# Attention's value products as plain float32 on halves of the array, row sums by ones on its quarters

## The chip, the cores and the metric

The kernel runs on one core of one Trainium2 chip. TensorE (PE, with its weight loader PEld) multiplies into PSUM, eight banks of 128 x 512 float32; VectorE (DVE) and ScalarE (ACT) read and write PSUM and SBUF; GpSimd (POOL) works on SBUF alone. Transfers (DMA) are issued from SyncE's queue (SP) or from GpSimd's. The metric is the device time of one execution in microseconds (us), the median of several runs.

## The reference: one layer for a prompt and eight short streams

One encoder layer is applied to a prompt of 2048 frames and to 8 streams of 16 new frames with 1024 cached ones. A modulated norm and one input projection give two groups of channels. Group A is a gated convolution of width 31 with a layer norm and a swish. Group B is attention with 8 heads of 64 channels and a forget gate: queries and keys are normed, and the logit of query t and key s has the sum of the log forget values between them added. The two are joined, projected and added to the input, and a gated feed-forward part follows. In the prompt's attention, cut to what matters:

```python
s = einsum('bqhd,bkhd->bhqk', q, k) * HEAD_DIM ** -0.5
s = s + (cum_q[..., :, None] - cum_k[..., None, :])
s = where(k_pos <= q_pos, s, -1e30)
p = softmax(s)
out = einsum('bhqk,bkhd->bqhd', p, v)
```

Everything is float32, and the results must have nearly float32's precision.

## The kernel before

**Two kinds of product.** A float32 operand can be given to TensorE as plain float32, or as fp32r, a reduced form that streams faster. Where the kernel wants speed and precision it splits an operand x into two fp32r halves, hi (ACT's copy of x) and lo = x - hi (DVE or GpSimd), and adds three products, hi*hi, hi*lo, lo*hi. The helper `parts_of` (lines 1158 to 1162) does the split, so the split of every operand appears in the profile under lines 1160 and 1161 and must be told apart by its tile name.

**Stages.** `project_u_v`, then `project_q_k` (norms, queries and keys, already split, go to the DRAM tensors `q_d` and `k_d`), `attention` (lines 778 to 827), `project_out`, and the feed-forward part `ffn_up` and `ffn_down`.

**Attention.** `STEPS` are 16 steps: 4 pairs of heads p, times 4 blocks qb of 512 queries. In a step, scores lie with the keys on the 128 partitions and the 512 queries along the row. A step has 4 * qb + 4 key tiles (kt) of 128 keys, for each of two heads h; the last four cross the diagonal, and only 512, 384, 256 and 128 of their query columns are computed. One score (a unit of the step's loop) is two fp32r products into a bank of the tag "u" (three banks), the first with the hi parts K1 and Q1, the second with K2 and Q2, which hold the rest and, in rows from `AUX` = 96, the maxima to be subtracted; a third product adds the mask on the diagonal.

`attend` (lines 954 to 1006) turns a score into weights: ACT's exp into `ef` (line 981), the split of `ef` into the two halves of `e` (line 986: ACT's copy, then DVE or, for every third, GpSimd), and later the products of `value` (lines 962 to 965): three fp32r products of 128 stationary columns for each head. The stationary operand is V's 64 channels beside 64 columns of ones, so each head has a bank of its own (tag "tr"), in which 64 rows are the result and 64 the row sums. V is split in `load` (lines 896 to 911). At the end of a step (lines 995 to 1006) ACT copies the four half banks out, computes 1 / sum as exp(-ln), DVE refines that in three operations, multiplies, and SP's queue stores into `cat_d`.

`score_maxima` (lines 913 to 943) runs ahead of the scores: for each 128 queries and 512 keys one product (line 934) into a bank of the tag "cv" (two banks) and one DVE maximum (line 937). `spread_maxima` (lines 945 to 952) transposes a step's maxima and multiplies them with a constant `bm` into Q2's aux rows (line 950). A score is pinned behind a maximum (lines 974 and 975): at least `AHEAD` = 32 and up to 40 ahead of its own number. `attention` emits 48 ahead (`LEAD`).

**Order of the work.** `weave` mixes the generators of a step: its scores, the loads for the next, the maxima, and from the third step on a slice of `background`: layer norms of the convolution (`conv_norm`) and then the streams' attention (`sample_setup`, `sample_batch`), all in one PSUM bank, "lane". They use plain float32 products, many of them on quarters of the array's columns with `tile_position` (lines 716, 1073, 1107). A scheduler with a timeline of its own puts each engine's instructions in order by priority; `later` shifts the priority (`MAXIMA_BY`, `BACK_BY`), and `after` pins one instruction behind another on one engine. Keys, queries (lines 889, 891, 903, 927) are loaded through GpSimd's queue; V and nearly all else through SP's. Both queues work in order: an issue that waits holds those behind it.

## Time and profile before

| | us |
|---|---|
| median of 3 runs | 2819.75 (2818.45 to 2822.88) |
| the profiled execution's own time | 2814.3 |
| its span, first to last instruction | 2812.5 |
| attention, first exp to last value product | 625.9 to 1197.6 |
| first product of the output projection | 1200.5 |

A row of a group reads: line, engine, operation, out <- in, shapes, count | busy us, mean ns of one | idle time of its engine ahead of it and what ended most of that. A plain float32 product is recorded as two MATMULs; "128*32" is the part of the array in rows and columns. A row of a timeline is the start, the time from there to the end of the merged instructions, and what they are. A row of waits is the waiting engine and line <- what released it: us in total, times, the longest. PE's busy time includes each product's way through the array after its last column has entered, so two products that follow each other overlap in it; the distance between starts tells what one costs.

### The profile page before, as it was taken

What the parts mean: (1) busy time and instruction counts of PE and PEld (TensorE: products, weight loads), DVE (VectorE), ACT (ScalarE), POOL (GpSimd) and SP (SyncE); (2) the same over time, 40 slices, a digit from 0 to 9 for tenths busy, and PEclk for the clock granted to TensorE, in tenths of its full rate; (3) what the DMA queues carried; (4) which work ended last, traced back from release to release, by engine and by line L of the source; (5) the groups of instructions that cost most, each with busy time, mean ns of one, the idle gap of its engine ahead of it and who ended that gap; (6) DMA issues with size and microseconds to landing.
All of it is one profiled execution on the core that took longest, in us unless ns stands there. A gap on an engine that the chain in (4) does not pass through costs nothing. (4 is left out here: it accounts for less than half of the span.)

```text
span 2812.5 us, 48566 instructions
## 1 busy us (share of the span) xinstructions
PE 2718.6 (97%) x16536; PEld 2515.7 (89%) x16536; DVE 2161.9 (77%) x4235; ACT 1428.7 (51%) x2812; POOL 503.9 (18%) x685
## 2 busy tenths in 40 slices
PE   7999999999989999999999999999999999999999
PEld 6999988866667777698999989999999999999999
DVE  2798898989888787546397989877887778666765
ACT  4443323357776777744354446444554446555552
POOL 3454411243333222214201110000000000000000
PEclk9999999979999999999999999999999999999999
DMA  8753657673334766365576869866786769788883
GB/s 325 249 192 107 191 209 267 182 204 109 101 95 128 203 179 189 130 215 179 181 259 209 294 215 308 268 221 218 233 287 214 226 190 319 244 284 257 271 255 116
DMA packets 389960, 599.24 MB, mean 213 GB/s; under 512 B 47136, under 2 KB 250048, under 8 KB 387664
## 3 DMA queue, kind: packets, MB, share of 16 engines
q1 hardware_dynamic: 375248, 570.73, 62.8%
q0 software_dynamic: 14464, 25.42, 3.9%
q8 instruction: 130, 2.13, 0.3%
q14 instruction: 118, 0.97, 0.1%
HBM read 421.97 MB, written 174.08 MB: 212 GB/s over the span
## 5 line engine op out<-in xcount | busy, mean ns | idle before, releaser
L1456 PE MATMUL z<-rT,rW 128*128 128x360 f32 (+1 forms) x8316 | 1383.3, 328 | 5.5 <-ACT rW L1160 1.4
L1456 PEld LDWEIGHTS z<-rT,rW 128*128 128x128 f32 x8316 | 1378.7, 188 | 8.1 <-ACT rW L1160 2.4
L1160 ACT ACTIVATE rW<-rR 128x512 fp32r<-128x512 f32 x714 | 434.4, 617 | 386.8 <-PE z L1456 272.1
L1161 DVE TENSOR_TENSOR rW<-rR,rW 128x512 fp32r<-128x512 f32 x714 | 479.5, 676 | 154.5 <-ACT rW L1160 151.3
L700 DVE SCALAR_TENSOR_TENSOR cv<-cu,cpar,cv 128x384 f32<-128x384 f32 x580 | 311.6, 614 | 2.8 <-ACT cv L698 2.8
L964 PE MATMUL pv<-e,V 128*128 128x512 f32 (+3 forms) x960 | 268.9, 388 | 14.1 <-DVE e L1161 6.3
L964 PEld LDWEIGHTS pv<-e,V 128*128 128x128 f32 x960 | 167.9, 194 | 71.7 <-DVE e L1161 14.6
L937 DVE TENSOR_REDUCE M<-mx 128x1 f32<-128x512 f32 (+2 forms) x320 | 188.7, 603 | 50.2 <-PE mx L934 31.7
L981 ACT ACTIVATE ef<-s 128x512 f32<-128x512 f32 (+3 forms) x320 | 167.1, 532 | 116.7 <-PE s L979 47.1
L512 PE MATMUL z<-hqx,wqh 128*128 128x384 f32 (+1 forms) x768 | 196.6, 333 | 1.0 <-DVE logf L347 1.0
L1160 ACT ACTIVATE rT<-traw 128x360 fp32r<-128x360 f32 (+1 forms) x315 | 149.1, 501 | 91.7 <-DMA traw<-gt_d 62.9
L1161 DVE TENSOR_TENSOR rT<-traw,rT 128x360 fp32r<-128x360 f32 (+1 forms) x315 | 157.6, 531 | 45.0 <-ACT rT L1160 44.7
L1161 POOL TENSOR_TENSOR e<-ef,e 128x512 fp32r<-128x512 f32 (+3 forms) x106 | 127.2, 1200 | 347.4 <-ACT e L1160 180.7
L1160 ACT ACTIVATE e<-ef 128x512 fp32r<-128x512 f32 (+3 forms) x320 | 175.5, 567 | 4.0
L1161 DVE TENSOR_TENSOR e<-ef,e 128x512 fp32r<-128x512 f32 (+3 forms) x214 | 149.1, 704 | 35.4 <-ACT e L1160 34.4
L512 PEld LDWEIGHTS z<-hqx,wqh 128*128 128x128 f32 x768 | 135.7, 188 | 18.9 <-issue 15.3
L934 PE MATMUL mx<-K,Q 96*128 96x512 f32 (+2 forms) x320 | 134.3, 427 | 17.5 <-DVE M L937 11.3
L1144 PE MATMUL acc<-ch,woh 128*128 128x360 f32 (+1 forms) x384 | 127.4, 333 | 10.0 <-ACT ch L1160 4.6
L1384 DVE TENSOR_TENSOR rR<-rR 128x512 f32<-128x512 f32 (+1 forms) x136 | 93.4, 707 | 50.9 <-DMA rR<-w_down 44.1
L973 PE MATMUL s<-Q,K 128*128 128x512 f32 (+3 forms) x320 | 125.8, 393 | 3.4 <-ACT ef L981 3.4
L1144 PE MATMUL acc<-ch,wol 128*128 128x360 f32 (+1 forms) x384 | 126.9, 331 | 0.0
L512 PE MATMUL z<-hqx,wql 128*128 128x384 f32 (+1 forms) x384 | 126.4, 329 | 0.0
(306 smaller groups left out, 3935.4 us busy)
## 6 DMA issues: line engine op xcount, KB each, us to landing
rR<-sup_d SPq DMA_DIRECT2D x176, 256.0 KB
rR<-w_gate SPq DMA_DIRECT2D x132, 256.0 KB
traw<-gt_d SPq DMA_DIRECT2D x154, 180.0 KB
rR<-w_down SPq DMA_DIRECT2D x104, 256.0 KB
rR<-sdn_d SPq DMA_DIRECT2D x96, 256.0 KB
rR<-w_up SPq DMA_DIRECT2D x88, 256.0 KB
sup_d<-rR SPq DMA_DIRECT2D x88, 256.0 KB
wa<-w_ada SPq DMA_DIRECT2D x16, 1024.0 KB
```

What stands on the lines that cost most here:

```text
L512: nc.tensor.matmul(z[:, :n], w[:, m], x[:, :n], start=(c == 0 and k == 0), stop=(c == CB - 1 and k == 2))
L700: self.pin(nc.vector.scalar_tensor_tensor(dst, src, w, acc[i], ALU.mult, ALU.add))
L934: self.mx.append(nc.tensor.matmul(mx[:, :w], Q2[0:AUX, h, j * P:(j + 1) * P], K2[kb][0:AUX, h, :w], start=True, stop=not diag))
L937: nc.vector.tensor_reduce(M[:, i, kb:kb + 1], mx[:, :w], AX.X, ALU.max)
L964: nc.tensor.matmul(z[h][:, off:], V[kt // 4][:, v, kt % 4, h:h + 2, :].rearrange("p b c -> p (b c)"), e[:, x, off:], start=(kt == 0 and i ...
L973: first = nc.tensor.matmul(s[:, off:], K1[kb][:, h, sl], Q1[:, h, off:], start=True, stop=False)
L981: self.last_piece = nc.scalar.activation(ef[:, off:], s[:, off:], AF.Exp)
L1144: self.nc.tensor.matmul(z[:, :n], w[:, m], y, start=(first and i == 0 and k == 0), stop=(last and i == len(terms) - 1 and k == 2))
L1160: copy = self.nc.scalar.activation(hi, raw, AF.Copy)
L1161: engine.tensor_tensor(lo, raw, f32(hi), ALU.subtract)
L1384: nc.vector.tensor_tensor(t, x, y, op)
L1456: nc.tensor.matmul(z, W[:, x, m], t[:, y, :w], start=(k == 0 and i == 0), stop=(k == n - 1 and i == 2))
```

## The change

- Value products: `e` is ACT's exp in float32, not split; V is loaded in float32 straight into its tile, not split. Per key tile one plain float32 product for each head, with 64 stationary columns, head 0 on the array's columns 0 to 63, head 1 on 64 to 127, into one bank.
- Row sums: after every second key tile, for the two tiles and the two heads, a plain float32 product with 32 columns of ones on one quarter of the array each (in steps with qb = 0 both tiles use the same two quarters), into a second bank.
- Order: the products of a key tile are pinned behind the scores of the key tile two later, sums behind products, the next scores and maxima behind those. The last products of a step run in the next step's first key tiles.
- End of a step: ACT copies the product bank (`zc`) and the sums (`sm`). Through GpSimd's queue the sums go to DRAM and come back with the 512 queries spread over the partitions, DVE adds and takes the reciprocal (in the next step, 8 scores later), they go to DRAM again and come back broadcast to 64 rows for each head; GpSimd multiplies, and its queue stores. The very last step instead spreads the sums by a product, and DVE takes the reciprocal of 128 x 512.
- Maxima: `spread_maxima` copies the transposed rows and sends 8 rows by SP's queue to row 96 of Q2, one aux row instead of 8; `bm` goes. `MAXIMA_BY` goes from -300 to 30, the lead from up to 40 to up to 42.
- Keys and queries are loaded through SP's queue instead of GpSimd's.
- Newton steps after exp(-ln/2): one instead of two, in `project_q_k` and `conv_norm`.
- Background: loads of cached keys and of the streams' bias are issued one piece earlier, more yields, and its first products are pinned behind a score's last product (`behind`).

```diff
-MAXIMA_BY, BACK_BY = -300, 1000
+MAXIMA_BY, BACK_BY = 30, 1000
...
-            newton_rsqrt(nc, y, zp.tile([P, NB], F32, tag="t", name="rt", bufs=1)[:, :n], v, 2, self.pin)
+            newton_rsqrt(nc, y, zp.tile([P, NB], F32, tag="t", name="rt", bufs=1)[:, :n], v, 1, self.pin)
...
-            nc.gpsimd.dma_start(K2[0:HD + 2], rows[HD:])
+            nc.sync.dma_start(f32(K2[0:HD + 2]), rows[HD:])
...
-            nc.gpsimd.dma_start(k1, rows[0:P])
+            nc.sync.dma_start(f32(k1), rows[0:P])
...
-        nc.gpsimd.dma_start(Q1, self.q_d[2 * p:2 * p + 2, :, t].rearrange("h r t -> r h t"))
+        nc.sync.dma_start(f32(Q1), self.q_d[2 * p:2 * p + 2, :, t].rearrange("h r t -> r h t"))
...
-        hi, lo = (v[:, i, :, 0:3:2, :] for i in range(2))
-        self.after(self.parts_of(hi, lo, raw.rearrange("p t (h e) -> p t h e", h=2), nc.vector), self.last_piece)
...
                     self.mx.append(nc.tensor.matmul(mx[:, :w], Q2[0:AUX, h, j * P:(j + 1) * P], K2[kb][0:AUX, h, :w], start=True, stop=not diag))
+                    if self.last_product:
+                        self.after(self.mx[-1], self.last_product)
...
-        for h in range(2):
-            nc.vector.tensor_tensor(Q2[r, h, :].rearrange("r (j q) -> r j q", j=4),
-                                    pz[r, :].unsqueeze(1).broadcast_to([8, 4, P]),
-                                    self.bm[r, h, :].unsqueeze(2).broadcast_to([8, 4, P]), ALU.mult)
+        m = self.lp.tile([P, P], F32R, tag="mrow", name="mrow", bufs=1)
+        nc.vector.tensor_copy(m[r], pz[r])
+        for i in range(8):
+            nc.sync.dma_start(f32(Q2[AUX:AUX + 1, i // 4, i % 4 * P:(i % 4 + 1) * P]), f32(m[AUX + i:AUX + i + 1]))
...
+        def values(kt, off, es):
+            if kt == 0:
+                z.append(self.bank("tr", "pv"))
+            for h in range(2):
+                product = nc.tensor.matmul(z[0][HD * h:HD * h + HD, off:], V[kt // 4][:, kt % 4, HD * h:HD * h + HD], es[h][:, off:],
+                                           start=(kt == 0), stop=(kt == nkt - 1), tile_position=(0, HD * h))
+                if h == 0:
+                    self.after(product, self.last_s)
+            self.last_product = product
+            sums.append((kt, off, es))
+            if kt % 2 == 0:
+                return
+            if kt == nkt - 1:
+                zc = wk.tile([P, 512], F32, tag="zc", name="zc")
+                self.last_exp = nc.scalar.copy(zc, z[0])
+            if kt == 1:
+                z.append(self.bank("tr", "sm"))
+            for k, o, x in sums:
+                part = k % 2 if qb else 0
+                for h in range(2):
+                    g = 2 * part + h
+                    self.last_product = nc.tensor.matmul(z[1][32 * g:32 * g + 32, o:], self.ones[:, 0:32], x[h][:, o:], start=(k == part),
+                                                         stop=(k == nkt - 1 or k == nkt - 2 and qb > 0), tile_position=(0, 32 * g))
+                    self.after(self.last_product, product)
...
-                at = min(self.nscore + AHEAD + min(self.nscore // 6, 8), len(self.mx) - 1)
+                at = min(self.nscore + AHEAD + min(self.nscore // 5, 10), len(self.mx) - 1)
                 self.after(first, self.mx[at])
+                if self.last_product:
+                    self.after(first, self.last_product)
...
-                ef = wk.tile([P, 512], F32, tag="ef", name="ef", bufs=3)
-                self.last_piece = nc.scalar.activation(ef[:, off:], s[:, off:], AF.Exp)
...
-                self.parts_of(e[:, 0, off:], e[:, 1, off:], ef[:, off:], nc.gpsimd if self.split3 == 0 else nc.vector)
...
+                e = wk.tile([P, 512], F32, tag="e", name="e", bufs=14)
+                self.last_piece = nc.scalar.activation(e[:, off:], s[:, off:], AF.Exp)
+                es.append(e)
+                if h:
+                    self.waiting.append((values, kt, off, es))
+                    if len(self.waiting) > 2:
+                        self.next_values()
+                if self.due and self.nscore >= self.due[0][0]:
+                    self.due.pop(0)[1]()
...
+    def end_of_step(self, p, qb, zc, sums):
...
+        self.last_exp = nc.scalar.copy(sm[r], sums[r])
...
+        if (p, qb) == STEPS[-1]:
+            spread = self.bank("cv", "R")
+            nc.tensor.matmul(spread, self.four, sm, start=True, stop=True)
+            nc.vector.reciprocal(R, spread)
+            nc.vector.tensor_tensor(zc, zc, R, ALU.mult)
+            nc.sync.dma_start(cat, zc)
+            return
+        queue = nc.gpsimd
+        for i in range(2 * parts):
+            queue.dma_start(self.sum_d[p, qb, i:i + 1], sm[32 * i:32 * i + 1])
+        w = wk.tile([P, 2, 2, 4], F32, tag="inv", name="inv")
+        queue.dma_start(w[:, 0:parts], self.sum_d[p, qb, 0:2 * parts].rearrange("(k h) (a c) -> a k h c", h=2, c=4))
+
+        def rest():
+            if qb:
+                self.after(nc.vector.tensor_tensor(w[:, 0], w[:, 0], w[:, 1], ALU.add), self.last_max)
+            self.after(nc.vector.reciprocal(w[:, 0], w[:, 0]), self.last_max)
+            queue.dma_start(self.inv_d[p, qb].rearrange("h (a c) -> a h c", c=4), w[:, 0])
+            for h in range(2):
+                queue.dma_start(R[HD * h:HD * h + HD], self.inv_d[p, qb, h:h + 1].broadcast_to([HD, 512]))
+            nc.gpsimd.tensor_tensor(zc, zc, R, ALU.mult)
+            queue.dma_start(cat, zc)
+
+        self.due.append((self.nscore + 8, rest))
```

More of the change, by code (lines that the diff above doesn't have):

```diff
@@ L715, in channel_mean @@
             for j in range(4):
-                nc.tensor.matmul(pm[32 * j:32 * j + 32, :n], self.ones[:, 0:32], src[j], start=True, stop=True,
+                self.behind(nc.tensor.matmul)(pm[32 * j:32 * j + 32, :n], self.ones[:, 0:32], src[j], start=True, stop=True,
                                  tile_position=(0, 32 * j))
@@ L800, in attention @@
         first = self.load(0)
-        next(first)
-        next(first)
+        drain(first)
         for n, (p, qb) in enumerate(STEPS):
@@ L860, in background @@
         bank = self.bank("ss", "lane")
-        more = self.after_attention.enter_context(self.pool(name="e2", bufs=1, side="right"))
-        self.eslots += [(more, f"e{i}") for i in range(5, 8)]
         with self.pool(name="cn", bufs=1) as cn:
@@ L957, in attend @@
         Q1, Q2 = self.Q1.pop(n), self.Q2[n % 4]
-        z = [self.bank("tr", "pv") for _ in range(2)]
         nkt = 4 * qb + 4
-        waiting = []
-        def value(kt, h, off, e):
-            for i, (v, x) in enumerate(((0, 0), (0, 1), (1, 0))):
-                nc.tensor.matmul(z[h][:, off:], V[kt // 4][:, v, kt % 4, h:h + 2, :].rearrange("p b c -> p (b c)"), e[:, x, off:],
-                                 start=(kt == 0 and i == 0), stop=(kt == nkt - 1 and i == 2))
+        z, sums = [], []
+        def values(kt, off, es):
[22 more added lines that the diff above has]
+                    self.after(self.last_product, product)
+            sums.clear()
+            if kt == nkt - 1:
+                self.end_of_step(p, qb, zc, z[1])
         for kt in range(nkt):
@@ L986, in attend @@
-                self.parts_of(e[:, 0, off:], e[:, 1, off:], ef[:, off:], nc.gpsimd if self.split3 == 0 else nc.vector)
-                waiting.append((kt, h, off, e))
-                if h and len(waiting) > len(self.eslots) - 3:
-                    value(*waiting.pop(0))
-                    value(*waiting.pop(0))
-                yield
-        for w in waiting:
-            value(*w)
-        pvs, sm = (wk.tile([P, 512], F32, tag=k, name=k, bufs=1) for k in ("pvs", "sm"))
-        for h in range(2):
-            o, x = slice(HD * h, HD * h + HD), slice(HD - HD * h, P - HD * h)
-            nc.scalar.copy(sm[o], z[h][x])
-            nc.scalar.copy(pvs[o], z[h][o])
@@ L1000, in attend @@
-        r = wk.tile([P, 512], F32, tag="rs", name="rs", bufs=1)
-        nc.scalar.activation(r, sm, AF.Ln)
-        self.last_exp = nc.scalar.activation(r, r, AF.Exp, scale=-1.0)
-        nc.vector.tensor_tensor(sm, sm, r, ALU.mult)
-        nc.vector.scalar_tensor_tensor(sm, sm, 2.0, r, ALU.subtract, ALU.mult)
-        nc.vector.scalar_tensor_tensor(pvs, pvs, -1.0, sm, ALU.mult, ALU.mult)
-        self.last_store = nc.sync.dma_start(self.cat_d[:, 4 + p, qb * 512:(qb + 1) * 512], pvs)
+                    self.last_s = nc.tensor.matmul(s[:, off:off + P], self.masks[:, 2], self.masks[:, 1], start=False, stop=True)
@@ L1008, in sample_setup, with behind, issue @@
+    def behind(self, op):
+        def issue(*args, **kw):
+            ins = op(*args, **kw)
+            self.after(ins, self.last_s)
+            return ins
+        return issue
     def sample_setup(self, bank):
@@ L1029, in sample_setup @@
         for kt in range(8):
-            nc.tensor.matmul(pt[:n, 2 * kt:2 * kt + 2], lf[:, kt, :], self.ones[:, 0:2], start=True, stop=True)
+            self.behind(nc.tensor.matmul)(pt[:n, 2 * kt:2 * kt + 2], lf[:, kt, :], self.ones[:, 0:2], start=True, stop=True)
         suf = sm.tile([P, 8], F32, name="suf")
@@ L1632, in host_layout @@
                             for w in range(2)], 1))
-    bm = np.zeros((P, 2, 4), np.float32)
-    for h in range(2):
-        for j in range(4):
-            bm[AUX + 4 * h + j, h, j] = 1
-    r["bm"] = bm
     r["sel"] = np.concatenate([
```

122 lines of the change are left out of this document (76 added, 46 removed).

## The prediction

> **What bounds the kernel now.** I read the page first, then the busy times by stage.
>
> ```profile
> span 2812.5 us, 48566 instructions
> PE 2718.6 (97%) x16536; PEld 2515.7 (89%) x16536; DVE 2161.9 (77%) x4235; ACT 1428.7 (51%) x2812; POOL 503.9 (18%) x685
> ```
>
> ```profile
> 1400.00:2812.00 1412.00, 1397.57 (x8425) 1393.76 (x8423) 1109.50 (x2157) 689.53 (x1347) 46.66 (x39) 0.99 0.75 244
> ```
>
> ```profile
> 626.00:800.00 174.00, 161.63 (x721) 116.72 (x722) 147.25 (x245) 129.99 (x258) 58.37 (x60) 0.95 0.40 107
> 800.00:1000.00 200.00, 183.19 (x1047) 139.61 (x1050) 162.09 (x290) 141.12 (x285) 59.50 (x56) 0.97 0.53 145
> 1000.00:1200.00 200.00, 188.41 (x1360) 140.57 (x1360) 144.05 (x248) 152.41 (x309) 50.62 (x48) 0.98 0.56 169
> ```
>
> The columns are: stretch, length, then busy us of PE, PEld, DVE, ACT and POOL with instruction counts, clock, DMA share, GB/s. Half of the span (1400 to 2812, the feed-forward part) is TensorE with its weight loader busy 1394 of 1412 us. The diff does not touch it. What the diff does touch is attention, 626 to 1200, 574 us. There the weight loader is busy 117 + 140 + 141 of 574 us, so the array has room although its busy column says 93%: that column counts each matmul's pipeline tail. DVE is busy 453 us (79%), ACT 424, POOL 168. So attention is bound by no single engine. I look next at what the array needs and what it waits for.
>
> ```profile
> L964 PE MATMUL pv<-e,V 128*128 128x512 f32 (+3 forms) x960 | 268.9, 388 | 14.1 <-DVE e L1161 6.3 <-POOL e L1161 3.6 <-ACT e L1160 3.6
> ...
> L1073 PE MATMUL lane<-kc,Qbd 128*32 128x512 f32 x128 | 17.6, 622 | 4.1 <-DVE S L1075 4.1
> L1107 PE MATMUL lane<-vc,pT 128*32 128x128 f32 x512 | 16.0, 274 | 0.0
> L716 PE MATMUL lane<-cq,ones 128*32 128x512 f32 (+1 forms) x40 | 15.3, 541 | 0.0
> L1089 PE MATMUL lane<-ident,S 128*128 128x128 f32 x64 | 10.2, 285 | 1.0 <-ACT S L1082 1.0
> L721 PE MATMUL lane<-cm,mean 128*128 128x512 f32 (+1 forms) x20 | 9.1, 539 | 0.0
> ```
>
> ```profile
> 879.67 0.40 PE L973 MATMUL s<-Q,K 128*128 128x512 f32 x1
> ...
> 880.14 1.31 PE L964 MATMUL pv<-e,V 128*128 128x512 f32 x5
> 881.28 0.39 PE L973 MATMUL s<-Q,K 128*128 128x512 f32 x1
> ...
> 919.32 0.27 PE L964 MATMUL pv<-e,V 128*128 128x128 f32 x1
> 919.53 1.06 PE L1073 MATMUL lane<-kc,Qbd 128*32 128x512 f32 x8
> 920.52 0.44 PE L964 MATMUL pv<-e,V 128*128 128x128 f32 x2
> 920.80 0.47 PE L934 MATMUL mx<-K,Q 96*128 96x512 f32 x1
> ```
>
> Five fp32r products of 512 columns start at 880.14 and the next matmul starts at 881.28: 0.228 us each, 0.445 ns a column. The code's loops give 417,792 columns of value products, 278,528 of scores, 139,264 of maxima and 32,768 of masks, 868,352 in all, and some 15,000 of the maxima run before 626: 853,000 x 0.445 ns = 380 us. The five lower rows, the background work in plain float32, add 68. So the array needs about 448 of 574 us and stands without work for about 126. The rows of its weight loader show ahead of what:
>
> ```profile
> L964 PEld LDWEIGHTS pv<-e,V 128*128 128x128 f32 x960 | 167.9, 194 | 71.7 <-DVE e L1161 14.6 <-issue 9.3 <-ACT e L1160 8.5
> L977 PEld LDWEIGHTS s<-Q,K 128*128 128x128 f32 x319 | 62.5, 196 | 9.2
> L973 PEld LDWEIGHTS s<-Q,K 128*128 128x128 f32 x319 | 62.4, 196 | 18.3 <-ACT ef L981 6.1 <-issue 2.2 <-ACT e L1160 1.7
> L934 PEld LDWEIGHTS mx<-K,Q 96*128 96x128 f32 x287 | 55.7, 195 | 41.5 <-DVE M L937 19.8 <-issue 6.5 <-DVE e L1161 3.7
> ```
>
> In the ratio 71.7 : 41.5 : 27.5 the 126 us are about 64 ahead of value products (they wait for the two halves of e), 37 ahead of maxima (they wait for DVE to empty a bank) and 25 ahead of scores.
>
> **What the value products cost.** Before, a key tile of full width takes 6 x 0.228 = 1.37 us for both heads. After, each head is one plain float32 product on 64 columns of the array, and the sums are further float32 products with ones on quarters. The trace has that kind: at 919.53 eight records, four float32 products on four quarters in two passes each, hold the array until 920.52, 0.99 us, although each alone would stream 2 x 0.427 = 0.853 us (four times the 0.213 us of 512 columns at the full clock). So the quarters run side by side. Ahead of them the array idles 0.15 us (the 128-column record at 919.32 takes 0.06 of the 0.21). I take 1.14 us for a visit of the two halves and 0.99 for a visit of the sums that follows it, once for two key tiles.
>
> - Off the diagonal lie 24 full-width key tiles per pair of heads, 96 in all, 48 pairs. A pair costs 2 x 1.14 + 0.99 = 3.27 us for 2.74 before: 157 us for 131.
> - A diagonal block of four tiles has 512 + 384 + 256 + 128 columns. Before: 6 x 1280 x 0.445 ns = 3.4 us. After: products 2.13 + 4 x 0.29 = 3.29, sums 1.28 + 2 x 0.14 = 1.56, or 2.41 in the four steps with qb = 0, where all sums share two quarters. 16 blocks: 53 + 19 + 10 = 82 us for 55.
>
> The array's need rises by (157 + 82) - (131 + 55) = about 53 us, to some 501. Its bounds: none of the visits costs more than its stream (about 57 us less: 160 visits x 0.29 + 80 x 0.14), or the halves do not run side by side (a rival below). I take the row, since it is this kind of instruction in this stage.
>
> The Trainium skill, TensorEngine Tiling (Array Packing), section Key Properties, says that changing the tiling mode drains TensorE; this speaks against the change, which makes five changes for two key tiles where there was none. The 0.15 us in and 0.14 us over the stream at 919.53 agree with it; by the rule the sum stays as it is, and without it the stage would be 57 us shorter.
>
> **What falls away beside it.** DVE and ACT in attention:
>
> ```profile
> L1161 DVE TENSOR_TENSOR e<-ef,e 128x512 fp32r<-128x512 f32 (+3 forms) x214 | 149.1, 704 | 35.4 <-ACT e L1160 34.4
> L950 DVE TENSOR_TENSOR Q<-pz,bm 8x512 fp32r<-8x512 f32 x28 | 18.3, 692 | 0.6 <-PE pz L948 0.2
> ...
> L1004 DVE SCALAR_TENSOR_TENSOR sm<-sm,rs 128x512 f32<-128x512 f32 x15 | 12.8, 850 | 0.0
> ...
> L1161 DVE TENSOR_TENSOR V<-vraw,V 128x512 fp32r<-128x512 f32 x16 | 12.4, 774 | 3.6 <-ACT V L1160 3.5
> ...
> L94 DVE SCALAR_TENSOR_TENSOR ct<-cr 128x512 f32<-128x512 f32 (+1 forms) x10 | 7.7, 766 | 0.1
> ```
>
> ```profile
> L1160 ACT ACTIVATE e<-ef 128x512 fp32r<-128x512 f32 (+3 forms) x320 | 175.5, 567 | 4.0
> ...
> L998 ACT COPY sm<-pv 64x512 f32<-64x512 f32 x32 | 18.6, 581 | 5.6 <-PE pv L964 4.9
> ...
> L1001 ACT ACTIVATE rs<-sm 128x512 f32<-128x512 f32 x16 | 10.0, 626 | 0.0
> ```
>
> DVE loses 149 (low halves of e), 18 (spreading the maxima), 3 x 12.8 (end of step), 12 (V) and half of 3 x 7.7 (one Newton step of two): 229 of 453 us, and gains some 8 of small copies: 40% of the stage. ACT loses 176, 19 (half of the end's copies), 20 (Ln and Exp) and 10 (V): from 424 to about 200. POOL loses its third of the low halves. Then a score's way to its product is one exp of 0.6 us, not exp, cast and subtraction, and the product stands two key tiles behind. I leave 6 of the 64 us ahead of value products. The 37 ahead of maxima halve with DVE's load (19). Of the 25 ahead of scores 16 stay, since the banks of s are still three. The stage: 501 + 41 = 542 us, 32 less than 574.
>
> **Edits at the edges and costed at nothing.** Ahead of attention, where the first maxima run, DVE works among others on these:
>
> ```profile
> 598.36 1.31 DVE L950 TENSOR_TENSOR Q<-pz,bm 8x512 fp32r<-8x512 f32 x2
> ...
> 610.61 0.42 DVE L94 SCALAR_TENSOR_TENSOR rt<-ry 128x256 f32<-128x256 f32 x1
> ```
>
> It loses there one Newton step (three such instructions) and two such spreads: I take -3 us, between 0 and -4. At the very end a reciprocal of 128x512 comes in:
>
> ```profile
> L600 DVE RECIPROCAL lfd<-lfd 128x32 f32<-128x32 f32 x3 | 1.1, 350 | 2.9 <-POOL lfd L599 2.9
> L600 DVE RECIPROCAL lfd<-lfd 128x8 f32<-128x8 f32 x1 | 0.2, 193 | 0.0
> ...
> 1200.49 0.67 PE L1144 MATMUL acc<-ch,woh 128*128 128x368 f32 x1 [2.60 <-ACT ch L1160]
> ```
>
> 6.5 ns an element give 3.5 us; with copy (0.6) and spread product (0.9) the bank is free 5 us after the sums. The next stage's first three accumulators cover 1.5, and the gap of 2.6 us at 1200.49 goes: +1 us, between -2 and +4. Ends of the other steps run through four transfers on POOL's queue (5.7 us each by the row below, nine issues) and a product on GpSimd: some 25 us behind the step. POOL's later transfers wait for the earlier ones, but nothing else of attention stands in its queue; zc has two buffers, and its rows are read only by the next stage. ACT's copy to zc waits for the step's last visit with the next exps behind it, about the length of the sums' visit, 1 us, while PE is in that visit. This cover would be gone if two steps together were shorter than the 25 us; the shortest two have 24 units of 1.8 us. The 64 loads of keys and queries move from POOL's queue to SP's, past the background's loads and stores, and 8 rows of maxima per step follow (128): costed at nothing as long as SP does not stand still, see below. The background's earlier loads save the 4.1 us wait of L1073; it is in the 25. The maxima's place in the order (48 ahead at most, 42 for 40) is costed at nothing for the same reason: DVE empties their banks sooner.
>
> Sum: -32 - 3 + 1 = -34. On the profiled execution, 2814.3 us (its span 2812.5 and 1.8 around it), 2780; the median of the runs lies 5.45 higher, 2819.75: 2786.
>
> **Rivals.** *Late operands on SP's queue.* SP is in order and stood behind slow work:
>
> ```profile
> SPq L906 <- DVE sm L1004: 166.2, 12, 30.5
> SPq L747 <- DVE cy L745: 53.4, 4, 19.5
> ...
> SPq L747 <- DVE e L1161: 23.8, 1, 23.8
> ...
> K<-k_d POOLq DMA_DIRECT2D x16, 512.0 KB, 5.7
> ```
>
> Nothing urgent was behind it then; now keys, queries and the maxima rows are. Maxima are emitted at most 48 ahead of the scores and must be 42 ahead, so 6 units of 574 / 320 = 1.8 us, 11 us, are the slack: a stall of SP beyond that comes through whole. The waits of 19.5 and 23.8 would give 8 + 13; and where the 16 steps' loads come just in time, 16 x 5.7 = 91 more, of which I take half. Against it: L906's long waits go with their shared buffer, and DVE, which caused them, is emptier. -34 + 21 + 46 = +33: 2853, slower. *The halves do not overlap.* Only quarters are shown side by side. 69,632 columns x 1.67 ns = 116 us more: 2902. The Trainium skill, TensorEngine Tiling (Array Packing), section Available Configurations, lists 128x64 as two tiles; no run here shows it. *The waits stay.* If the array's idle time comes from the order of its queue rather than from e, 90 of the 126 remain beside the higher need: 591, +15: 2835. *Nearly full array.* With 10 us of waiting left: 511: 2755.
>
> **How the numbers follow.** Forecast 0.56, with its own range of 2765 to 2805 (waiting 20 to 60 us); nearly full array or cheaper visits 0.17; waits stay 0.10; late operands 0.12; halves 0.05. About 0.2% (5.6 us) is what a measurement can tell from no change. Faster takes the first two and a little of the third: 0.75; same 0.05; slower 0.20. The range goes from 2745 (a nearly full array, and a fifth of the 57 us off the visits) to 2828 (most of the way to the waits that stay); it leaves out the last two and the rest of the third.
>
> **What would show it.** Right: value records in pairs a few ns apart, pass to pass 0.43 us, a visit of 1.1 us; no L1160 or L1161 rows of e; DVE in attention near 225 us; the stage 520 to 560 us with PEld waits ahead of mx halved; no change after 1400. Wrong: passes of the second half starting 0.85 us behind the first; PE waits named DMA Q or DMA K; long waits of SP at step starts; a clock under 0.95 in the stage; or the stage shorter than 500 us, which would mean that the visits cost less than their row.

## The result and the profile after

The kernel after takes 2803.89 us (median of 5 runs, 2800.88 to 2813.40) against 2819.75 before (2818.45 to 2822.88): ratio 0.9949, 95% interval 0.9927 to 0.9971, some 16 us faster. The forecast was 34 us faster. Its profiled execution, 2813.4 us, is the slowest of its five, so the same kernel was run again (experiment 1, profiled at 2804.5 us), and both traces are used.

The head of the page of after, and its busy times by stage (columns as in the prediction):

```profile
span 2811.6 us, 48409 instructions
PE 2741.7 (98%) x16858; PEld 2391.7 (85%) x16858; DVE 1951.1 (69%) x3936; ACT 1237.5 (44%) x2406; POOL 424.0 (15%) x662
```

```profile
626.00:800.00 174.00, 172.16 (x863) 83.76 (x863) 93.08 (x172) 75.61 (x147) 31.67 (x48) 0.98 0.43 129
800.00:1000.00 200.00, 198.15 (x1286) 99.22 (x1285) 94.10 (x201) 79.11 (x156) 37.47 (x58) 1.00 0.58 170
1000.00:1200.00 200.00, 191.12 (x1294) 89.67 (x1293) 68.78 (x132) 80.39 (x153) 29.01 (x44) 0.97 0.51 148
```

```profile
1400.00:2811.00 1411.00, 1396.55 (x8423) 1393.54 (x8421) 1110.01 (x2157) 689.53 (x1347) 46.47 (x39) 0.99 0.75 244
```

The feed-forward part did not move. In attention the load of the other engines fell, by most of what was forecast: DVE from 453 to 256 us (forecast 225), ACT from 424 to 235 (forecast 200), POOL from 168 to 98. And PE, busy 93% before, is now busy 561 of 574 us. So 200 us of DVE's work went, and the time moved by 16. Where the rest stayed is the question. These are the starts of the events that bound the stages, read off the timelines (us, all of them starts; "stage" is from the first exp to the last value or sums product, "tail" from there to the first product of the output projection, "projection" from there to the first feed-forward product):

| trace | first exp | last value product | first projection | first feed-forward | stage | tail | projection |
|---|---|---|---|---|---|---|---|
| before | 625.9 | 1197.6 | 1200.5 | 1407.2 | 571.7 | 2.9 | 206.7 |
| after | 622.2 | 1185.9 | 1198.6 | 1406.9 | 563.7 | 12.8 | 208.3 |
| after, again | 619.6 | 1174.1 | 1187.1 | 1397.9 | 554.5 | 13.0 | 210.8 |

From before to the second trace of after: start -6, stage -17, tail +10, projection +4, and nothing after it: -9.7 us, as the two spans say (2812.5 and 2802.8). It is less than the 16 us of the medians, because the profiled execution of before lies 5.5 us below its median and this one of after 1.6 above. The stage got half of its forecast 32 in this trace and a quarter in the first one (8.0), and the tail, forecast at +1, took 10 back.

**Inside the stage.** PE starts one product after another, so the time from each start to the next can be added up by what the first of the two is. What lies between two starts is not all the first one's, though: it holds PE's idle time ahead of the second as well. Here this idle time is taken out and stands in a row of its own (sums over the instructions of the two traces; the forecast's need is 186 + 194 + 68, its waits 126).

| us of the stage | before | after, again | change | forecast |
|---|---|---|---|---|
| value products and sums | 224.6 | 217.7 | -6.9 | +53 (186 to 239) |
| maxima, with masks and pz | 82.7 | 93.1 | +10.4 | 0 |
| scores, with masks | 153.9 | 167.6 | +13.7 | 0 |
| background | 71.7 | 73.2 | +1.5 | 0 |
| PE idle, all of it | 38.7 | 2.8 | -35.9 | -85 (126 to 41) |

The stage's -17 is the sum of these rows. Before, the array was taken up for 533 us and not for 448, and the profile shows 39 us of idle, not 126. (Ends of products are modelled, so a wait shorter than a product's way through the array can hide in the upper rows.) Nearly all of the idle time went, and products whose code did not change, the maxima and the scores, became 24 us dearer. The timeline of PE in after shows why (start, us, engine, line, operation):

```profile
1002.77 0.39 PE L996 MATMUL s<-Q,K 128*128 128x512 f32 x1
1003.09 1.08 PE L959 MATMUL pv<-e,V 128*64 128x512 f32 x4
1004.10 0.50 PE L923 MATMUL mx<-K,Q 96*128 96x512 f32 x1
1004.44 0.40 PE L990 MATMUL s<-Q,K 128*128 128x512 f32 x1
...
1007.14 1.07 PE L976 MATMUL sm<-e,ones 128*32 128x512 f32 x8
1008.13 0.50 PE L923 MATMUL mx<-K,Q 96*128 96x512 f32 x1
1008.48 0.39 PE L990 MATMUL s<-Q,K 128*128 128x512 f32 x1
1008.71 0.39 PE L996 MATMUL s<-Q,K 128*128 128x512 f32 x1
```

A visit of the two halves lasts from 1003.09 to 1004.10, 1.01 us, a visit of the sums 0.99. The single records behind the first line start in twos, 7 ns apart: the halves run side by side. Two passes of 0.427 us would be 0.85; the first takes 0.05 more, and behind the last come 0.10: over the whole stage the median from a last pass to the next fp32r product is 0.522 instead of 0.427. The way in is charged to the product ahead: the median from a last score to the first value product is 0.326 us where 0.233 is usual, and 153 visits follow a score or its mask, 14 us. Then there is a part that the forecast lacked: from 1004.10 to 1004.44 is 0.34 us, and from 1008.13 to 1008.48 0.35, for a product that otherwise takes 0.23 (1008.48 to 1008.71). The first product after a visit costs 0.1 us more; 112 visits are followed by a maximum or a score, 11 us. These 25 us, an estimate from counts and medians, are about what maxima and scores rose by. The weight loader's timeline of the same stretch shows how:

```profile
1000.54 0.19 PEld L990 LDWEIGHTS s<-Q,K 128*128 128x128 f32 x1 [0.84 <-issue]
...
1003.09 0.20 PEld L959 LDWEIGHTS pv<-e,V 128*64 128x64 f32 x4 [0.35 <-issue]
1004.10 0.19 PEld L923 LDWEIGHTS mx<-K,Q 96*128 96x128 f32 x1 [0.81 <-DVE M L928]
1004.21 0.19 PEld L990 LDWEIGHTS s<-Q,K 128*128 128x128 f32 x1
1004.44 0.19 PEld L996 LDWEIGHTS s<-Q,K 128*128 128x128 f32 x1
```

In the stream a product's weights load while the product before it runs: those of L996 at 1004.44, where L990's product starts. After the visit the loader has stood 0.81 us, and the weights of the first product load at 1004.10, not ahead of it. That line names DVE as what ended the wait, but at 1000.54, after a visit of the sums, the loader stands as long with no wait named, and the first product again takes 0.33 us. Loads follow each other at 0.11 us (1004.10, 1004.21), which is about the missing tenth. In all a visit pays 0.09 + 0.05 + 0.10 + 0.10 = 0.34 us beyond its stream. The Trainium skill states under TensorEngine Tiling (Array Packing), section Key Properties, that changing the tiling mode drains TensorE; the 0.09 and 0.10 us at the two ends agree with it, and the tenth behind it comes on top.

**The clock.** The 533 us of before are not all taken up at the same speed. In one stretch the granted clock is 0.50 (columns as above), and there products of 512 columns start 0.43 us apart instead of 0.23:

```profile
869.50:876.00 6.50, 6.23 (x23) 4.70 (x23) 2.49 (x4) 2.76 (x6) 2.60 (x3) 0.50 0.00 0
```

```profile
869.77 0.65 PE L716 MATMUL lane<-cy,ones 128*32 128x128 f32 x8 [2.16 <-DMA cy<-y_d]
...
871.37 0.63 PE L973 MATMUL s<-Q,K 128*128 128x512 f32 x1
871.80 0.63 PE L977 MATMUL s<-Q,K 128*128 128x512 f32 x1
```

The wait of 2.16 us that ends at 869.77 lies around the start of this stretch; what lowers the clock was not tested. By the clock record of the traces, 38.5 us of the stage ran at 0.5 before, 17.3 in the first trace of after and 7.7 in the second; over the stage the mean clock is 0.97, 0.98 and 0.99. Compared with like products at the full clock, some 10 us of the stage's -17 are this (an estimate). The forecast had no term for it, and no run here changes the clock alone.

### The profile page after: what moved, and what is told of

The parts are those of the page before. It is cut to its first block, busy times and chain, and to the rows that moved or that the text cites. A ratio compares the mean times of both kernels' runs of the same rounds, so it can differ in the third digit from the quotient of the medians.

```text
span 2811.6 us, 48409 instructions
## 1 busy us (share of the span) xinstructions
PE 2741.7 (98%) x16858; PEld 2391.7 (85%) x16858; DVE 1951.1 (69%) x3936; ACT 1237.5 (44%) x2406; POOL 424.0 (15%) x662
## 4 chain that ended last, share of the span: by engine, by line
PE 53%; DMA 1%; DVE 1%; POOL 0%; issue 0%; ACT 0%; SPq 0%; DVEq 0%; POOLq 0%; ACTq 0%
PE z L1537 48%; PE acc L1225 5%; DMA traw<-ht_d 0%; DMA cr<-cat_d 0%; POOL xo L1350 0%; DMA xo<-xT 0%; DVE rT L1242 0%; DMA ht_d<-xo 0%; DVE cl L1242 0%; PE pr L1334 0%; DVE xo L1233 0%; POOL nx L1350 0%; DVE rR L1465 0%; DVE rW L1242 0%; PE pr L1322 0%
## 5 line engine op out<-in xcount | busy, mean ns | idle before, releaser
L1000 ACT ACTIVATE e<-s 128x512 f32<-128x512 f32 (+3 forms) x320 | 169.1, 533 | 296.3 <-PE s L996 166.0
L923 PEld LDWEIGHTS mx<-K,Q 96*128 96x128 f32 x320 | 62.3, 196 | 115.6 <-issue 53.0
L959 PE MATMUL pv<-e,V 128*64 128x512 f32 (+3 forms) x640 | 156.1, 558 | 0.0
L923 PE MATMUL mx<-K,Q 96*128 96x512 f32 (+2 forms) x320 | 144.3, 459 | 11.8 <-DVE M L928 6.1
L990 PE MATMUL s<-Q,K 128*128 128x512 f32 (+3 forms) x320 | 126.6, 396 | 0.0
L1225 PE MATMUL acc<-cl,woh 128*128 128x360 f32 (+1 forms) x384 | 122.4, 330 | 0.0
L996 PE MATMUL s<-Q,K 128*128 128x512 f32 (+3 forms) x320 | 118.4, 370 | 0.0
L342 PE MATMUL pvv<-wvh,hx 128*128 128x260 f32 x544 | 101.2, 286 | 3.9 <-ACT v L346 3.9
```

The costliest lines, as they stand in the source:

```text
L923: self.mx.append(nc.tensor.matmul(mx[:, :w], Q2[0:AUX, h, j * P:(j + 1) * P], K2[kb][0:AUX, h, :w], start=True, stop=not diag))
L959: product = nc.tensor.matmul(z[0][HD * h:HD * h + HD, off:], V[kt // 4][:, kt % 4, HD * h:HD * h + HD], es[h][:, off:], start=(kt == 0), s ...
L990: first = nc.tensor.matmul(s[:, off:], K1[kb][:, h, sl], Q1[:, h, off:], start=True, stop=False)
L996: self.last_s = nc.tensor.matmul(s[:, off:], K2[kb][:, h, sl], Q2[:, h, off:], start=False, stop=not diag)
L1000: self.last_piece = nc.scalar.activation(e[:, off:], s[:, off:], AF.Exp)
L1225: self.nc.tensor.matmul(z[:, :n], w[:, m], y, start=(first and i == 0 and k == 0), stop=(last and i == len(terms) - 1 and k == 2))
```

## The experiments

**1. After, unchanged.**

> The changed kernel as it is, once more, for a second profile and more times. Theory (the array is full through attention, and what it spends there is set by the visits to the float32 products): the stage from first exp to last sums takes 550 to 566 us again, ratio to before 0.993 to 0.997. Rival (the gain is eaten by late operands on SP's queue, which vary from run to run): a profile of a quicker execution shows the same visits and a stage shorter by 8 us or more, with fewer waits named DMA Q or K.

Measured: 2802.94 us, ratio 0.9957 (0.9942 to 0.9972), runs from 2799 to 2818. What follows: the result repeats; after spreads more than before. The run does not decide between the theory and its rival: the stage is in the theory's range, but it is also 9 us shorter than in the first trace, and PE's waits for loads of queries (DMA Q) are 1.3 us instead of 5.2. In all PE's idle time is 2.8 us for 7.5, and of the rest, 4 us, the smaller share at half clock is enough. The rows by group of PE in this trace (busy us, mean ns | idle us ahead of it and what ended it), and below them those of before that were not shown yet:

```profile
L959 PE MATMUL pv<-e,V 128*64 128x512 f32 (+3 forms) x640 | 154.3, 554 | 0.0
L923 PE MATMUL mx<-K,Q 96*128 96x512 f32 (+2 forms) x283 | 124.9, 446 | 2.5 <-DMA Q<-q_d 1.3 <-DVE M L928 1.0
L990 PE MATMUL s<-Q,K 128*128 128x512 f32 (+2 forms) x315 | 123.5, 392 | 0.0
L996 PE MATMUL s<-Q,K 128*128 128x512 f32 (+2 forms) x315 | 115.3, 366 | 0.0
L976 PE MATMUL sm<-e,ones 128*32 128x512 f32 (+3 forms) x640 | 83.3, 540 | 0.0
```

```profile
L973 PE MATMUL s<-Q,K 128*128 128x512 f32 (+2 forms) x319 | 125.0, 392 | 3.4 <-ACT ef L981 3.4
L934 PE MATMUL mx<-K,Q 96*128 96x512 f32 (+2 forms) x287 | 116.8, 412 | 13.4 <-DVE M L937 8.8 <-DMA Q<-q_d 2.8 <-DVE Q L950 1.5
```

By the idle column the waits did go: 14.1 to 0.0 ahead of value products, 13.4 to 2.5 ahead of maxima, 3.4 to 0.0 ahead of scores. But it also says how little there was to gain ahead of the last two: 17 us by PE's idle time, not the 62 that the forecast put there. And a maximum itself became dearer, 446 ns for 412.

**2. Sums twice.** Is the array full? All products with ones are made twice, so that the sums double and the attention's result is half of the reference's:

```
-            for k, o, x in sums:
+            for again, (k, o, x) in ((i, y) for i in range(2) for y in sums):
```

(with start and stop on the first and the last of them).

> Every product with ones is done twice (the sums are twice too large, so the result is half): the work of the sums is doubled, in the same visits. Theory (array full): all of the added streaming is paid, 80 visits with 65 us in all, so +62 to +70 us against the changed kernel, ratio to before 1.017 to 1.020. Rival (the array has slack, some other engine or queue sets the pace): clearly under 45 us, ratio under 1.011.

Measured: 2875.26 us, ratio 1.0206 (1.0191 to 1.0221), 72 us above after on the same chip, a little more than the theory's 62 to 70. Its row of sums:

```profile
L976 PE MATMUL sm<-e,ones 128*32 128x512 f32 (+3 forms) x1280 | 153.4, 539 | 0.0
```

From start to start the sums take 142.6 us for 74.8, +68, and the stage grows by as much and more. Nothing of the added work finds a free place: in attention of after the array has no room left. Whether it had some before, as the forecast read it, was not tested this way.

**3. Two key tiles in one visit.** Half of the visits of the halves, same products:

```
-                    if len(self.waiting) > 2:
+                    if kt % 2 and len(self.waiting) > 3:
+                        self.next_values()
                         self.next_values()
```

> Value products of two key tiles in one visit, so 80 visits fewer; nothing else changes. In the changed kernel's profile a visit costs about 0.09 us on the way in (0.326 us from the last score to the first product, 0.233 else), 0.095 on the way out (0.522 for a pass of 0.427) and 0.1 on the first fp32r product after it (0.334 for 0.233). Theory (array full, visits dear): 80 x 0.29 = 23 us less, ratio to before about 0.987. Rival (the stage waits for transfers, maxima or exps): within 5 us of the changed kernel, 0.993 to 0.997; or slower, since four scores in a row need more than the three banks.

Measured: 2805.40 us, 0.9957 (0.9945 to 0.9969), no difference to after. But the stage changed inside. Without idle time, value products and sums take 202.7 us for 217.7, scores 164.0 for 167.6: with the maxima (92.7 for 93.1) 19 us less for 80 visits fewer, 0.24 us each. PE's idle time takes it back, 20.1 us for 2.8, and the background takes 4.1 more. The largest of PE's waits is that ahead of the layer norms' products; here it is in this trace, then in that of experiment 1 (us in total, times, longest):

```profile
PE lane L1056 <- DMA cy<-y_d: 9.9, 3, 5.1
```

```profile
PE lane L1055 <- DMA cy<-y_d: 0.3, 1, 0.3
```

In this order a background product reaches the array before its rows have come from memory, and everything behind it in PE's order stands.

**4. The same, with the rows earlier.** To 3 are added five pieces of the background's order instead of two between the load of y and its first product (the count of its pieces follows), and the background ends earlier (`BACK` 0.75 for 0.85):

```
-        yield
-        yield
+        for _ in range(5):
+            yield
```

> Value products of two key tiles in one visit, as before, and two things that were seen to stand in the way of it: the layer norms' products wait three pieces longer after their load is issued (PE had stood 1 to 5 us each time for the rows of y, 11 us in all), and the background is to be done at 75%. Theory (a visit costs 0.29 us beyond its stream, and what the paired kernel saved was lost to the background's operands and to the tail): 15 to 25 us less than the changed kernel, ratio to before 0.986 to 0.991. Rival (visits cost nothing that shorter runs of scores would not lose elsewhere): ratio 0.993 or more.

Measured: 2790.47 us, 0.9912 (0.9897 to 0.9927). The stage is 543.5 us, the wait for y 2.4 us for 9.9. Without idle time the value group takes 205.4, scores 162.1, maxima 90.9: 20 us less than in experiment 1, the 19 of experiment 3 again. With fewer waits in its place (15.1 us of idle for 20.1) the price of the visits is seen as time. How much of the 13 us below after is theirs is not shown, since three things were changed and only the pairs and `BACK` (experiment 6) ran alone. The tail is 12.6 still.

**5. The tail: the last store on GpSimd's queue.** The tail in the timeline of after:

```profile
1185.62 0.63 PE L976 MATMUL sm<-e,ones 128*32 128x256 f32 x8
...
1186.98 1.13 PE L1029 MATMUL R<-sm,four 128*128 128x512 f32 x2 [0.61 <-ACT sm L1024]
1188.20 3.36 DVE L1030 RECIPROCAL aR<-R 128x512 f32<-128x512 f32 x1
1188.24 1.28 ACT L1163 ACT_TABLE_LOAD   x1
1190.84 0.66 PE L1170 MATMUL lane<-ident,S 128*128 128x128 f32 x4 [2.73 <-ACT S L1163]
1192.32 0.35 SPq L1032 DMA_DIRECT2D cat_d<-zc  x1
1192.76 1.84 SPq L1277 DMA_DIRECT2D cr<-cat_d  x4
1194.47 3.64 PE L1188 MATMUL lane<-vc,pT 128*32 128x128 f32 x64 [0.34 <-ACT pTn L1178]
1198.62 0.68 PE L1225 MATMUL acc<-ch,woh 128*128 128x368 f32 x1
```

Two chains end together. The store of the last step waits on SP for the reciprocal, and the loads of the projection (cr) stand behind it in order, though they want rows of other blocks; and the last batch of the background runs by itself, softmax, transposes and 64 products, with a table load on ACT in it. The waits of SP's queue name the first:

```profile
SPq L1032 <- DVE zc L1031: 23.1, 1, 23.1
```

The edit is one word: `nc.gpsimd.dma_start(cat, zc)` for `nc.sync.dma_start(cat, zc)`.

> The very last step's store goes through GpSimd's queue instead of SP's, so that the output projection's loads do not stand behind it (SP waited 23 us for that store in the profile, and the first accumulating product came 12.4 us after the last sums, 2.9 before the change). Theory A (the gap is the queue): 4 to 7 us less than the changed kernel, ratio about 0.992 to 0.993. Theory B (the gap is the background's last batch, which ends at the same time): less than 2 us.

Measured: 2806.54 us, 0.9962 (0.9950 to 0.9973), tail 13.4: nothing. The second chain is as long, which experiments 6 and 7 bear out.

**6. The tail: the background ends earlier.** `BACK` 0.75 for 0.85 alone.

> One number of the changed kernel: the background is to be done after 75% of the scores, not 85%. In three profiles of the changed kernel the output projection starts 12.8 to 13.4 us after the last sums, and in that gap the last batch of the streams runs its chain of softmax, transposes and products alone; moving the last store off SP's queue left the gap as it was. Theory (the tail is the background's last batch): the gap falls to 3 to 6 us and the time by 5 to 9, ratio about 0.993. Rival (the gap is the end of the last step itself: copy, spread product, reciprocal): gap and time as they are.

Measured: 2827.21 us, 1.0037 (1.0024 to 1.0051), 23 us slower than after, where the theory had 5 to 9 less. The batch is out of the tail, and the tail is 11.4 us, nearly as long as in after, now with the store alone in it:

```profile
1198.52 3.36 DVE L1030 RECIPROCAL aR<-R 128x512 f32<-128x512 f32 x1 [0.92 <-PE R L1029]
...
1203.13 0.38 SPq L1032 DMA_DIRECT2D cat_d<-zc  x1
1204.59 1.80 SPq L1277 DMA_DIRECT2D cr<-cat_d  x4
...
1207.56 0.68 PE L1225 MATMUL acc<-ch,woh 128*128 128x368 f32 x1 [9.02 <-ACT ch L1241]
```

And the stage, which now has the batch in it, takes 575.6 us, 21 more than the second trace of after.

**7. Both.** `BACK` 0.75 with the last store and the four stores of catS on GpSimd's queue.

> The changed kernel with the background due at 75% (as in the run before, which came out 24 us above the changed kernel) and, besides, the last step's store and the four stores of the streams' results on GpSimd's queue, so that the output projection's loads no longer stand behind them on SP's. In that run the projection still started 11.4 us after the last sums although the background was through: its first operand was loaded only after those stores, which waited for the reciprocal of 3.4 us. Theory (the tail has two causes, each hidden behind the other: the last batch, and the loads behind the last stores): the gap falls to 3 to 5 us, 6 to 8 us less than the run with 75% alone, ratio to before about 1.001. Rival (something else holds the projection, such as a PSUM bank): gap of 9 us or more.

Measured: 2815.16 us, 0.9995 (0.9983 to 1.0006). The tail is 2.9 us, as before the change:

```profile
1199.52 0.63 PE L976 MATMUL sm<-e,ones 128*32 128x256 f32 x8
...
1202.71 0.43 PE L1225 MATMUL acc<-ch,woh 128*128 128x368 f32 x1 [0.58 <-ACT ch L1241]
```

So the tail has two causes, each hidden behind the other, and only removing both shows them. The stage, 579.0, took more than the tail gave back. Of its growth, some 24 us over the second trace of after, about 10 would be the chain that left the tail, whose products now queue with the others (an estimate from the tail's own fall). The clock fits the rest: 31.7 us of this stage ran at 0.5, for 7.7, worth some 11 us by the distance of its products (an estimate). In experiment 6, with 19.1 us at 0.5, PE also waits 4.7 us for a load of queries.

**8. Loads of keys and queries back on GpSimd's queue.** The forecast put the move of these 64 loads at nothing, with a rival in which it loses 67 us. In after, `nc.gpsimd` for `nc.sync` in the four places.

> The changed kernel with the 64 loads of keys and queries back on GpSimd's queue; all else as changed. Theory (array full; SP's waits cost at most the 1 to 5 us that PE shows as waits named DMA Q): within 5 us of the changed kernel, ratio to before 0.994 to 0.998. Rival (late operands on SP's queue eat part of the gain): 8 us or more less than the changed kernel, ratio under 0.993.

Measured: 2819.15 us, 1.0010 (0.9999 to 1.0021): all of the gain of the change is gone, some 15 us, which neither the theory nor the rival had. The waits of GpSimd's queue in this trace say what the loads do to it:

```profile
POOL sum_d L1036 <- ACT sm L1024: 86.1, 12, 14.5
POOL inv_d L1044 <- DVE inv L1043: 80.7, 13, 17.5
POOL Q L896 <- PE s L998: 47.1, 9, 14.3
...
POOL K L884 <- PE s L996: 40.9, 5, 12.1
```

A load waits up to 14 us for its buffer and holds up the ends of steps, and an end waits up to 17.5 us for its sums and holds up the loads. In the stage PE is idle for 13.2 us, 2.8 in experiment 1.

**9. Only the loads, in the kernel before.** The same 64 loads on SP's queue in before, nothing else.

> The kernel before with its 64 loads of keys and queries on SP's queue, and nothing else of the change. With them back on GpSimd's queue the changed kernel was 14 us slower. Theory A (the move pays because in the changed kernel the ends of steps stand in GpSimd's queue, so it belongs to the change and is worth little alone): within 4 us of the kernel before, or slower, since in it SP waits up to 30 us for the buffer of V; ratio 0.999 to 1.005. Theory B (the move is worth its 14 us by itself, and the float32 products bring next to nothing): 8 us or more less, ratio under 0.997.

Measured: 2809.23 us, 0.9966 (0.9955 to 0.9978): 10 us faster. The waits of GpSimd's queue in before, where these loads stood in one order with the third part of the low halves:

```profile
POOL Q L903 <- PE s L979: 25.6, 9, 5.3
...
POOL K L891 <- PE s L977: 13.8, 6, 3.8
```

39 us in which GpSimd split no e. What this did to PE is less plain. Its rows in this trace, to be held against those of before in the prediction (14.1 us of idle ahead of value products) and in experiment 1 (13.4 ahead of maxima):

```profile
L964 PE MATMUL pv<-e,V 128*128 128x512 f32 (+3 forms) x960 | 264.8, 386 | 17.8 <-DVE e L1161 11.8 <-ACT pvs L999 2.2 <-POOL e L1161 2.1
L934 PE MATMUL mx<-K,Q 96*128 96x512 f32 (+2 forms) x287 | 117.3, 412 | 4.2 <-DVE M L937 2.0 <-DVE Q L950 1.9
```

The wait ahead of maxima fell by 9 us, the waits for GpSimd's e by 1.5 alone (3.6 before), and those for DVE's e rose by 5.5. The stage is 8 us shorter. That the loads cost 10 us in GpSimd's queue is shown; by which wait is not.

**10. Only one Newton step, in the kernel before.** The 2 at the end of the two calls of `newton_rsqrt` becomes 1.

> The kernel before with one Newton step instead of two, in both places, and nothing else of the change. Forecast: -1 to -4 us through an earlier first exp (622 to 625 us instead of 625.9), ratio 0.9985 to 1.000. Rival: no effect that can be measured, since the last block's steps lie beside other waits.

Measured: 2811.21 us, 0.9986 (0.9975 to 0.9997): 4 us faster; the first exp comes at 622.8 instead of 625.9.

**11. Both of these, in the kernel before.**

> The kernel before with both small parts of the change: loads of keys and queries on SP's queue, one Newton step. Alone they gave 0.9966 and 0.9986. Theory (they add, and the float32 products with all that belongs to them net next to nothing): ratio 0.994 to 0.997, within 4 us of the changed kernel. Rival (both relieve the same wait, and the products carry part of the gain): ratio 0.9965 or more, 5 us or more above the changed kernel.

Measured: 2801.01 us, 0.9932 (0.9919 to 0.9944): 19 us faster, as much as the whole change or more, and no value product has changed.

**12. The rest alone.** After, with the loads on GpSimd's queue and two Newton steps.

> The other half: the changed kernel with the loads on GpSimd's queue and two Newton steps, so the products, sums, ends of steps, maxima rows and background as changed. Loads on GpSimd's queue alone gave 1.001. Theory (the products net next to nothing, within what the array's extra work and the tail take back): ratio 1.000 to 1.004. Rival (the loads matter only because of the ends of steps in the same queue, and Newton's steps nothing): ratio 0.9985 to 1.001, the same as with the loads alone.

Measured: 2817.15 us, 0.9989 (0.9975 to 1.0003): no difference to before that can be told. What names the change, the products, the sums and the new ends of steps, nets to next to nothing. Its trace (2826.1 us, 9 above the median) shows the two sides: PE's idle time in the stage falls from 38.7 to 17.9 us, its products take 19 us more, 25 of them in maxima and scores, so the stage is 1.6 shorter; and the tail is 7.5 longer.

**13. What the experiments point to.** Experiment 4 with the stores of experiment 7, once with `BACK` 0.75:

> Two key tiles in one visit, layer norms' products later, background due at 75%, last stores on GpSimd's queue. Without the last of these it took 2790 us with a gap of 12.6 us, 6 of it a wait for the first operand. Theory: the gap falls to 5 to 7 us, the time to 2782 to 2786, ratio about 0.989. Rival (the stores don't hold the projection): within 2 us of 2790.

Measured: 2782.99 us, 0.9884 (0.9871 to 0.9898), 33 us faster than before and the fastest of all; stage 539.4, tail 6.7. And with 0.85:

> The same with the background due at 85%, as in the changed kernel. Theory (the array is full, so work moved within attention costs the same there, and what counts is that the last batch doesn't run alone): the last batch runs alone again, gap 10 to 13 us, 3 to 8 us above the one with 75%. Rival (75% crowds the stage, as the run of the changed kernel with 75% may say: +24 us): 5 us or more below the one with 75%.

Measured: 2804.38 us, 0.9955 (0.9942 to 0.9968). Here the last value product is at 1162.4, but batches of the background go on until 1192.9, and the first feed-forward product comes at 1392.2 for 1376.1. So with the pairs the closer packing gains 21 us, for 3 to 8 expected, and without them (experiment 6) it costs 23. A reading is that the shorter attention leaves batches over; no further run shows it.

## Why the prediction was right and wrong, step by step

The kernel is faster, as forecast, but by 16 us and not 34, and mostly for another reason: the loads, put at nothing, and the Newton step, put at -3, alone give 19 (experiment 11), and everything else, forecast at -31, gives nothing that can be told from no change (experiment 12). That the direction came right is luck more than forecast.

**Array need 448, waits 126: wrong, and the root of the rest.** The columns times 0.445 ns are right for a stream of long products. What lay beyond was all called waiting and shared out by the loader's idle times. The loader's idle is not the array's: the loader also stands while an unlike visit or a long product runs. PE was taken up for 533 us and idle for 39, of which 14.1, 13.4 and 3.4 ahead of the three kinds; the row of value products with the first of these was in the prediction. So 36 us of idle went, not 85. Of the 85 us between 448 and 533, some 13 are half clock (an estimate); the rest, short products, changes of shape and waits too short to show, is not split further.

**The need rises by 53: wrong, +19.** Before, the value products took 225 us of the array and not 186; after, 218, and 232 with the way in, for 239 forecast. The price of the new form was nearly right and that of the old one 39 us too low. Two errors, in the need and in the waits, cancel in part, and the stage's -17 for -32 is what they leave.

**Visits at 1.14 and 0.99 us: right in kind, their return left out.** The halves run side by side; measured are 1.01 and 0.99 us, the first 1.10 with its way in. The tenth of a microsecond on the first product after a visit was in none of the terms, some 11 us on maxima and scores. A sign of it stood in the prediction's rows: at 920.52 two products of 128 columns took 0.28 us, where such products take 0.06 to 0.11 each elsewhere in the stage.

**Waits ahead of maxima halve with DVE's load: the wait went, its size and its test were wrong.** This was to be read from the loader:

```profile
L923 PEld LDWEIGHTS mx<-K,Q 96*128 96x128 f32 x284 | 53.8, 191 | 104.1 <-issue 52.3 <-DVE M L928 28.5 <-DVE inv L1043 3.3
```

It rose from 41.5 to 104.1 us, half of it "issue", while PE ahead of the same maxima stood 6.4 us in that trace. The loader stands during the visits. As a test this row was badly chosen; as a step, 11 us of PE's idle time went (13.4 to 2.5) where 18 were forecast, and the maxima rose by 10 of themselves.

**Waits ahead of value products 64 to 6: right that they go, 64 is not shown.** No idle is left ahead of L959, and DVE and ACT fell by most of what was worked out; PE's own idle there had been 14.1.

**Start -3: right, or a little small.** -4 and -6 in the two traces of after, and experiment 10 gives 3 of it to the Newton step.

**End +1, between -2 and +4: wrong, +10.** The reciprocal was priced well (3.36 us, forecast 3.5). What was missed is what stands behind it: the projection's first loads in SP's order behind the store that waits for it, and the background's last batch, which now ran by itself. Both had to go for the tail to close.

**Loads moved to SP, costed at nothing: wrong, -10.** The prediction asked what the loads meet in the new queue, and not whom they leave alone in the old one. The rival of late operands has the opposite sign: in the first trace of after PE waits 5.2 us in all for queries, in the second 1.3.

**Ends of steps hidden: right in after.** No wait of PE names them there; with the loads on GpSimd's queue (experiment 12) PE waits 5.1 us for ACT's copy to zc.

**The rivals.** That the halves do not overlap is excluded by the 7 ns; the two tiles that the Trainium skill lists under TensorEngine Tiling (Array Packing), section Available Configurations, are in the trace. That the array is nearly full is what came, by experiment 2, but at a need of 552 us, not 501. That the waits stay did not come: they went, and prices stand in their place. The sign of a clock under 0.95 did not come either; it rose. The forecast's stage of 542 us was reached, at 543.5, 539.4 and 542.2, only in experiments 4 and 13.

**Open:** what of the 533 us was price and what short waits, which wait the loads lengthened in GpSimd's queue, what the higher clock by itself is worth, the 4 us by which the projection lasts longer in the second trace, and why after spreads more from run to run.

## What to carry to other kernels

Time beyond the stream is not all waiting: add up PE from start to start by kind, take its idle time out, and take as removable only what a named engine ended. Look at the granted clock of the stage before comparing prices. When a change adds visits of another shape, price the way in, the way out and the first product back, and then look at what reaches the array late once it is faster. And a transfer that changes its queue has two prices, one in the queue it joins and one in the queue it leaves; here the second was most of the measured gain.

## What the runs showed of the hardware

Two plain float32 products on 64 columns each start 7 ns apart and stream 512 columns in 0.43 us a pass, two passes each. A visit of such a shape between fp32r products costs 0.09 us in, 0.05 us in its first pass, 0.10 us out and 0.10 us on the first product after it; 80 visits fewer took 19 us off the time that products take. In before, at a granted clock of 0.50, fp32r products of 512 columns start 0.43 us apart instead of 0.23. A reciprocal of 128x512 takes 3.36 us on DVE, and a table load on ACT 1.28 us.
